# Down projection of a gated feed-forward part: plain blocks and Strassen's seven products, in an encoder trunk of two layers

## The chip, the core and the metric

The kernel runs on one core of one Trainium2 chip. Its time is the device time of one execution in microseconds; the median of three runs before the change is 1561.34 us (1561.25 to 1561.52). The core's engines work side by side and wait for each other by semaphores: TensorE (PE; its weight loads are shown as PEld), VectorE (DVE), ScalarE (ACT), GpSimd (POOL), and SyncE (SP), which here issues nearly all DMAs. Matmuls write their sums into eight PSUM buffers of 128 partitions x 512 float32; the other working memory is SBUF.

## What is computed

The input x has 512 tokens of 1024 channels, and two layers follow each other. Each has three attention or pooling branches, which the change leaves alone, and a feed-forward part:

```python
x = x + merged @ w_out[l]
hf = rms_norm(x, ffn_norm_g[l])
u = depthwise_conv(hf @ ffn_w_up[l], ffn_conv_w[l], ffn_conv_b[l])   # width 3, along the tokens
u_gate, u_val = u[..., :D_FF], u[..., D_FF:]                          # D_FF = 2816
x = x + (jax.nn.silu(u_gate) * u_val) @ ffn_w_down[l]                 # 2816 -> 1024
```

All of it is float32. The kernel keeps that precision by splitting each operand of a matmul into a high part (rounded to TensorE's float32r) and a low part (the remainder), and by adding three matmuls: high x high, high x low, low x high.

## The kernel before

Everything lies transposed: channels on the 128 partitions, the 512 tokens along the row. The residual is the tile `XM` (8 row tiles of 128 channels), its normed and split form `HH` and `HL`.

**Weights.** The host packs all weights into one stream of pieces of up to 512 columns, in the order of use. `w_dma` loads two pieces at a time into one of three buffers `raw` (512 KB, on SP's queue). `w_split` makes of a piece the high part `wh` (a copy on ACT, line 248) and the low part `wl` (a subtraction on POOL, at times on DVE, line 256); `wnext` hands out the next piece and sees to it that three more are prepared.

**Up projection.** 2816 = 22 column tiles of 128 for the gate (part 0) and as many for the value (part 1). Each of the 44 takes 8 x 3 matmuls of 512 columns (`mm3`, line 405) into one PSUM buffer out of six (`acc`, `ST`, `AV`, two each). `up_evac` follows: DVE scales the result by the norm into an SBUF tile `u`; ACT forms the middle tap of the convolution in `a`; DVE adds the two outer taps (two instructions on `a` and `u`, line 260); then comes silu on ACT for the gate, or the product with the gate on DVE for the value, and the split into `ah` (ACT) and `al` (POOL). 22 pairs `ah`, `al` are kept until the down projection.

**Down projection.** For each of 8 row tiles m, 22 x 3 matmuls of 512 columns add up in one buffer; DVE adds the buffer to `XM`, and the result is stored. In layer 0 the next layer's norm is begun on it (`HH` on ACT, `HL` on DVE, squares on ACT, their sum on POOL); in layer 1 it is the output. Only the last row tile of layer 1 is cut into two halves of 256 tokens, in two buffers (`mi`, `S`), so that one half is stored while the other is still computed.

**Order.** Each engine runs its instructions in the order in which the program was written. That order comes from a planner in the program: `chain` lists the steps of one piece of work with what they wait for, and a model of the engines' times (`Clock`, `Engine`) decides how the steps of different chains follow each other.

Of the kernel before, what the change touches and what calls it, by code (L numbers as in the profile page):

```python
# [10 lines left out]
F32 = mybir.dt.float32  # L11
# [30 lines left out]
END = object()  # L42

# [42 lines left out]
def _widths():  # L86
# [10 lines left out]
    return r + [T] * (2 * KC) + [T] * (4 * FC) + [T] * (2 * FC)  # L97

# [191 lines left out]
def trunk(ctx: ExitStack, tc: tile.TileContext, x, w, prm, gb, cst, pad, out):  # L290
# [60 lines left out]
    raws, halves, pool_only = {}, {}, [False]  # L351

# [29 lines left out]

    def pick(bias, t=0.0):
# [9 lines left out]
    def w_ahead(j):  # L393
        while st["split"] <= min(j, len(pieces) - 1):
            w_split()

    def wnext():
        j = st["use"]
        w_ahead(j + LA if j > LA else j)
        st["use"] += 1  # L400
        need(("w", j))
# [28 lines left out]
    MQ, MK = [[cp.tile([P, 4, 4, 96], F32, tag=f"{n}{g}", name=f"{n}{g}") for g in range(2)] for n in ("MQ", "MK")]  # L430
# [144 lines left out]
    def layer(l, sq, xsrc):  # L575
        pr = prms[l]
        G1, G2 = 2 * l, 2 * l + 1

# [1080 lines left out]
        act = {}  # L1659
        gated = {}  # L1660
        fin = {}

        def up_evac(c, part, acc, tag):
            ci = c + part * FC
            u, a = slot("u"), slot("a")

            def scale():
                V.tensor_tensor(u[:, :T], acc, fin["rbc"][:, :T], ALU.mult)
                free(tag)
# [8 lines left out]
                                               ALU.mult, ALU.add)]  # L1678
            if part == 0:
# [4 lines left out]
                steps.append(gate)  # L1684
            else:
                ah, al = slot("ah", F32R), slot("al", F32R)
                act[c] = (ah, al)
# [3 lines left out]
                steps += [([("gate", l, c)], prod), *split(ah[:, :T], al[:, :T], a[:, :T], eng=G),  # L1691
                          lambda: done("act", l, c)]
            chain(*steps)

        n = 0
        norm_begin(G2, sq)
        for c in range(FC):
            for part in range(2):
                tag = tags[n % 3]
                n += 1  # L1700
                acc = ps(tag)
                for i, _ in enumerate(feat_major(acc, G2)):
                    norm_finish(G2, fin, n == 3 and i == 6)
                up_evac(c, part, acc, tag)

        last = l == L - 1
        sq = None if last else slot("sq")
        idx, tail = 0, []
        two = [ps(t) for t in ("mi", "S")] if last else None

        def half(n, kc, wh, wl):
            ts = slice(256 * n, 256 * n + 256)
            mm3(two[n][:, :256], wh, wl, act[kc][0][:, ts], act[kc][1][:, ts], kc == 0, kc == FC - 1)

        def out_half(n):
            ts = slice(256 * n, 256 * n + 256)
# [229 lines left out]
```

## Time and profile before

| | |
|---|---|
| median of three runs | 1561.34 us |
| the profiled execution, and its span | 1560.56 us, 1558.8 us |
| PE busy | 1547.1 us (99%), 7034 matmuls |
| DVE, ACT, POOL busy | 991.3, 790.6, 1038.5 us |
| layer 0: up projection, down projection | 421 to 661.3 us, 661.3 to 781 us |
| layer 1: up projection, down projection | 1195 to 1434.7 us, 1434.7 us to the end |
| granted TensorE clock | 1.0 |

The profile names an instruction by its line in the program, its engine, its output and inputs (buffer numbers left out) and their shapes. Lines of helpers stand for many uses: 405 is every split matmul, 256 every two-operand instruction of DVE or POOL. The rows that matter are shown where they are used.

### The profile page before, as it was taken

How to read it: one execution, taken by the hardware profiler on the slowest of the kernel's cores; microseconds unless marked ns; L12 is line 12 of the kernel's file. 1: busy time of each engine (PE TensorE's matmuls, PEld its weight loads, DVE VectorE, ACT ScalarE, POOL GpSimd, SP SyncE). 2: the span in 40 equal slices, each digit the busy share in tenths (PEclk: the TensorE clock that was granted, in tenths of full speed). 3: DMA queues.
4: the chain of work that ended last, by engine and by line, in shares of the span. 5: the costliest groups of instructions: out<-in, count | busy, mean ns of one | idle time of the engine just before them, and what ended most of it. 6: DMA issues, size and time to landing. Idle time of an engine off the chain costs nothing.

```text
span 1558.8 us, 20414 instructions
## 1 busy us (share of the span) xinstructions
PE 1547.1 (99%) x7034; PEld 1286.1 (83%) x7034; DVE 991.3 (64%) x1470; ACT 790.6 (51%) x1459; POOL 1038.5 (67%) x920
## 2 busy tenths in 40 slices
PE   9999999999999999999999999999999999999999
PEld 8888788888888888888898877888888888888888
DVE  6778889986277777711046788899762877776000
ACT  6557776663444444432244587766533544444221
POOL 4865986854766666664578669878547676666542
PEclk9999999999999999999999999999999999999999
DMA  6432234425323233333335322444243232322331
GB/s 216 122 107 74 75 104 133 130 80 155 101 82 109 95 95 96 94 122 113 110 109 132 109 69 68 128 126 133 79 144 95 95 102 88 108 95 95 108 131 46
DMA packets 82855, 166.46 MB, mean 107 GB/s; under 512 B 20928, under 2 KB 42944, under 8 KB 82752
## 3 DMA queue, kind: packets, MB, share of 16 engines
q1 hardware_dynamic: 82464, 165.03, 34.1%
q8 instruction: 55, 0.90, 0.2%
q14 instruction: 48, 0.39, 0.1%
q10 hardware_dynamic: 288, 0.14, 0.0%
HBM read 151.50 MB, written 13.63 MB: 106 GB/s over the span
## 4 chain that ended last, share of the span: by engine, by line
PE 89%; ACT 3%; DVE 3%; POOL 3%; issue 1%; DMA 0%; SPq 0%; POOLq 0%; ACTq 0%; DVEq 0%
PE ps_acc L405 39%; PE ps_AV L405 22%; PE ps_ST L405 20%; PE ps_S L405 2%; PE ps_mi L405 2%; PE ps_ST L1365 1%; POOL qa L256 1%; DVE XM L256 1%; ACT ps_ST L248 1%; DVE mgl L256 0%; POOL oraw L256 0%; ACT wh L248 0%; PE ps_ST L1323 0%; PE ps_mi L1365 0%; ACT qa L248 0%
## 5 line engine op out<-in xcount | busy, mean ns | idle before, releaser
L256 POOL TENSOR_TENSOR wl<-raw,wh 128x512 fp32r<-128x512 f32 (+3 forms) x501 | 672.3, 1353 | 382.9 <-ACT wh L248 342.0
L248 ACT ACTIVATE wh<-raw 128x512 fp32r<-128x512 f32 (+2 forms) x521 | 309.1, 608 | 128.7 <-PE ps_ST L405 43.5
L260 DVE SCALAR_TENSOR_TENSOR a<-u,prm,a 128x511 f32<-128x511 f32 x176 | 248.5, 1415 | 86.9 <-ACT a L248 80.6
L405 PE MATMUL ps_acc<-HH,wh 128*128 128x512 f32 x592 | 230.9, 390 | 0.0
L405 PE MATMUL ps_acc<-HL,wh 128*128 128x512 f32 x592 | 230.7, 390 | 0.0
L405 PE MATMUL ps_acc<-HH,wl 128*128 128x512 f32 x592 | 230.6, 389 | 0.0
L405 PEld LDWEIGHTS ps_acc<-HH,wl 128*128 128x128 f32 x592 | 111.1, 188 | 23.3
L405 PEld LDWEIGHTS ps_acc<-HH,wh 128*128 128x128 f32 x592 | 111.2, 188 | 23.2 <-DVE gt L256 0.6
L405 PEld LDWEIGHTS ps_acc<-HL,wh 128*128 128x128 f32 x592 | 111.2, 188 | 22.5
L405 PE MATMUL ps_AV<-HH,wh 128*128 128x512 f32 x288 | 112.3, 390 | 0.0
L405 PE MATMUL ps_AV<-HH,wl 128*128 128x512 f32 x288 | 112.1, 389 | 0.0
L405 PE MATMUL ps_AV<-HL,wh 128*128 128x512 f32 x288 | 112.1, 389 | 0.0
L256 POOL TENSOR_TENSOR al<-a,ah 128x512 fp32r<-128x512 f32 x44 | 59.9, 1360 | 76.8 <-ACT ah L248 74.7
L405 PE MATMUL ps_ST<-HH,wh 128*128 128x512 f32 x240 | 93.5, 390 | 0.0
L405 PE MATMUL ps_ST<-HL,wh 128*128 128x512 f32 x240 | 93.4, 389 | 0.0
L405 PE MATMUL ps_ST<-HH,wl 128*128 128x512 f32 x240 | 93.4, 389 | 0.0
L248 ACT ACTIVATE ah<-a 128x512 fp32r<-128x512 f32 x44 | 27.8, 632 | 121.0 <-DVE a L256 121.0
L248 ACT ACTIVATE a<-u,prm 128x512 f32<-128x512 f32 x88 | 71.0, 809 | 26.2 <-DVE u L256 25.5
L248 ACT ACTIVATE a<-a 128x512 f32<-128x512 f32 x44 | 27.6, 632 | 108.8 <-DVE a L260 108.8
L248 ACT ACTIVATE HH<-XM,prm 128x512 fp32r<-128x512 f32 x32 | 23.1, 722 | 102.5 <-DVE XM L256 53.9
L405 PEld LDWEIGHTS ps_AV<-HH,wl 128*128 128x128 f32 x288 | 54.1, 188 | 11.3
L405 PEld LDWEIGHTS ps_AV<-HH,wh 128*128 128x128 f32 x288 | 54.1, 188 | 11.1
(414 smaller groups left out, 3751.0 us busy)
## 6 DMA issues: line engine op xcount, KB each, us to landing
raw<-w SPq DMA_DIRECT2D x228, 512.0 KB, 3.5
raw<-w SPq DMA_DIRECT2D x13, 384.0 KB, 3.0
XM<-x SPq DMA_DIRECT2D x16, 256.0 KB, 3.7
dtq<-tr SPq DMA_DIRECT2D x16, 192.0 KB, 1.9
dtk<-tr SPq DMA_DIRECT2D x16, 192.0 KB, 2.0
tf<-dtq SPq DMA_DIRECT2D x48, 64.0 KB, 2.1
tf<-dtk SPq DMA_DIRECT2D x48, 64.0 KB, 2.3
raw<-w SPq DMA_DIRECT2D x6, 448.0 KB, 3.3
```

Source lines behind the costliest of these rows:

```text
L248: return self.eng.activation(out, in_, func, **k)
L256: return self.eng.tensor_tensor(out, *a)
L260: return self.eng.scalar_tensor_tensor(out, *a)
L405: PE.matmul(o, lhsT=lhsT, rhs=rhs, start=start, stop=stop)
L1365: PE.matmul(sc, lhsT=s[a_][:, kb_], rhs=s[b_][:, :T], start=False, stop=n == len(pairs) - 1, skip_group_check=True)
```

## The change

**Seven products.** Rows and contraction tiles of the down projection are taken in pairs, and the tokens in halves of 256. A piece of weights now holds a 2 x 2 block of 128 x 128 tiles (the host lays it out so). From the four blocks and four blocks of activations (two contraction tiles x two halves of tokens), seven products are formed in place of eight, each as three matmuls of 256 columns (`products`, line 1832 after). They add up over the contraction in four PSUM buffers per row pair; `unite` then forms the sums of the products and adds them to `XM`.

**Sums of weights** (`w_seven`): four of seven left factors are sums of blocks. ACT copies one block into a PSUM buffer (`mi` or `S`, in turn), three DVE instructions (256, 128 and 128 columns) form the sums there, ACT copies the 512 columns to a second `wh`, DVE subtracts for a second `wl`. The first `wh` and `wl` have 384 columns, since the fourth block is used only in sums. Pieces are prepared two ahead (`wnext`).

**Sums of activations** (`up_evac`): for every second column tile, DVE and POOL form the sums of activations, and three tiles of 512 and half of one are split per pair.

**Convolution out of PSUM**: the scaled value stays in the PSUM buffer (`u = acc`) in place of an SBUF tile, and the buffer is freed only behind the outer taps.

**Two halves**: column tiles 0 to 11 go up, and down as a partial sum, then tiles 12 to 21. One up tile of the second half (tile 12, part 0) runs ahead of the first half's products. The tiles `MQ`, `MK` of the attention serve as room for activations. The cut of the last row tile is gone: rows 6 and 7 end together.

```diff
+HALVES = ((0, 12), (12, 22))
+def _ups(c0, c1):
+    r = [(c, part) for c in range(c0, c1) for part in range(2)]
+    return r[c0 > 0:] + ([(c1, 0)] if c1 < FC else [])
...
+    def w_seven():
...
+        s = sums[j % 2]
+        a12, a11, a21 = (r[:, n * P:n * P + P] for n in (0, 2, 3))
+        s1, s2, s4 = (s[:, n * P:n * P + P] for n in (0, 2, 3))
+        def first():
+            A.activation(s2, a21, AF.Copy)
+            done("a21", j)
+            A.activation(his[0][:, :384], r[:, :384], AF.Copy)
+        def rest():
+            e = pick(W_BIAS)
+            e.tensor_tensor(los[0][:, :384], r[:, :384], f(his[0][:, :384]), ALU.subtract)
...
+        def both():
+            V.tensor_tensor(s[:, :256].rearrange("p (a b) -> p a b", a=2), s2[:, None, :].to_broadcast([P, 2, P]),
+                            r[:, P:3 * P].rearrange("p (a b) -> p a b", a=2), ALU.subtract)
+        def third():
+            V.tensor_tensor(s2, a11, s1, ALU.subtract)
+        def fourth():
+            V.tensor_tensor(s4, a12, s2, ALU.subtract)
+        def lo():
+            V.tensor_tensor(los[1], s, f(his[1]), ALU.subtract)
+            done("w", j)
+        chain(([("w", j - 2)] if seven[j - 2] else [], first), rest, after=0.0)
+        chain(([("a21", j)], both), third, fourth, lambda: A.activation(his[1], s, AF.Copy), lo, after=0.01)
...
         def up_evac(c, part, acc, tag):
-            u, a = slot("u"), slot("a")
+            u, a = acc, slot("a")
             def scale():
-                V.tensor_tensor(u[:, :T], acc, fin["rbc"][:, :T], ALU.mult)
-                free(tag)
+                V.tensor_tensor(u, acc, fin["rbc"][:, :T], ALU.mult)
...
+            def turns():
+                eng = V if c + 1 in (HALVES[0][1], HALVES[1][1]) else G
+                w0 = whole.pop(p)
+                chain(diff(t3, b22, w0[:, 256:T], ALU.add), diff(t4, b21, t2), qfree,
+                      *split(new[4][:, :T], new[5][:, :T], t34[:, :T], eng=eng), end(2), after=0.0)
+                chain(*split(new[2][:, :T], new[3][:, :T], t12[:, :T], eng=eng), end(1), after=0.0)
+            w0 = whole[p]
+            chain(([("first", l, p)], lambda: G.tensor_tensor(t1, w0[:, 256:T], w0[:, :256], ALU.subtract)), after=0.5)
+            chain(*steps, ([("gate", l, c)], prod), diff(t2, b22, t1, ALU.add), turns,
+                  *split(new[0][:, :T], new[1][:, :T], q), lambda: (done("act", l, p, 0), qfree()))
+        def products(kp, m, banks_, first):
...
+            bank_ = {2: (0, 0), 3: (0, 1), 1: (1, 0), 6: (1, 1), 4: (2, 0), 5: (2, 1), 7: (3, 0)}
+            left_ = {1: (0, 2), 2: (0, 0), 3: (1, 3), 4: (0, 1), 5: (1, 0), 6: (1, 2), 7: (1, 1)}
...
+            for n in (2, 1, 3, 6, 5, 4, 7):
...
+                for q, (x_, y_) in enumerate(((lh, rh), (lh, rl), (ll, rh))):
+                    PE.matmul(o, lhsT=x_, rhs=y_, start=first and b not in seen and q == 0, stop=False, skip_group_check=True)
...
+        def unite(m, banks_, then):
...
+            rush = then is not None and l == L - 1 and m == KC - 2
+            e = V if rush else G
+            chain(lambda: A.activation(p1, b1[:, :256], AF.Copy), after=0.0)
+            chain(add(x0, x0, b0), lambda: free(t0), add(u2, p1, b1[:, hi_]), lambda: free(t1),
+                  add(x0[:, hi_], x0[:, hi_], b2[:, hi_]), add(x1, x1, b2), lambda: free(t2),
+                  add(u3, u2, b3[:, :256]), lambda: free(t3),
+                  add(x0, x0, u[:, :T], e), lambda: then and then(m),
+                  lambda: e.tensor_tensor(pair(x1), pair(x1), u3[:, None, :].to_broadcast([P, 2, 256]), ALU.add),
+                  lambda: then and then(m + 1), after=0.0)
...
+        for c0, c1 in HALVES:
+            for c, part in _ups(c0, c1):
...
+            for m in range(0, KC, 2):
+                banks_ = {}
+                for k in range(c0, c1, 2):
+                    products(k // 2, m, banks_, k == c0)
+                unite(m, banks_, finish if c1 == FC else None)
```

**How the order moves.** TensorE, the first matmuls of layer 0's down projection, before: each takes the 512 columns of one activation tile, and 66 in a row go into one buffer (`ps_acc_6580`; `ah`, `al` are the parts of a column tile, `wh`, `wl` those of the weights).

```order
L405 MATMUL ps_acc_6580<-ah_4721,wh_6512 128x512
L405 MATMUL ps_acc_6580<-al_4722,wh_6512 128x512
L405 MATMUL ps_acc_6580<-ah_4721,wl_6513 128x512
L405 MATMUL ps_acc_6580<-ah_4813,wh_6512 128x512
L405 MATMUL ps_acc_6580<-al_4814,wh_6512 128x512
L405 MATMUL ps_acc_6580<-ah_4813,wl_6513 128x512
```

The same place in the change, the first four products of the first half (`sMK`, `sMQ` are activations in the attention's old room; `wh_0` and `wl_0` are the blocks as they are, `wh_1` and `wl_1` the sums; x2 stands for two halves of one tile).

```order
L1832 MATMUL ps_ST_5810<-sMK_4635,wh_0_5701 128x256
L1832 MATMUL ps_ST_5810<-sMK_4634,wh_0_5701 128x256
L1832 MATMUL ps_ST_5810<-sMK_4635,wl_0_5703 128x256
L1832 MATMUL ps_AV_5816<-sMK_4635,wh_0_5701 128x256 x2
L1832 MATMUL ps_AV_5816<-sMK_4635,wl_0_5703 128x256
L1832 MATMUL ps_ST_5810<-sMK_4635,wh_1_5702 128x256
L1832 MATMUL ps_ST_5810<-sMK_4634,wh_1_5702 128x256
L1832 MATMUL ps_ST_5810<-sMK_4635,wl_1_5704 128x256
L1832 MATMUL ps_AV_5816<-sMK_4634,wh_1_5702 128x256 x2
L1832 MATMUL ps_AV_5816<-sMK_4634,wl_1_5704 128x256
```

One matmul over 512 columns has become matmuls over 256 that go round four buffers; in all 990 wide and 132 narrow ones give way to 1848 narrow ones. The sums of weights are needed from the third product on.

VectorE behind layer 0's second up stage, in the change: `ps_ST_7538` is the last product of gate and value, `t_910`, `t_911` the sums of activations, `ah` the low parts of their splits, `ps_mi` and `ps_S` the sums of weights; `wl_1_7592` is the low part of the sums of piece 3, counted from 0.

```order
L272 TENSOR_TENSOR ps_ST_7538<-a_7537,a_7494 128x512
L272 TENSOR_TENSOR ps_mi_4767<-raw_7454,ps_mi_4767 128x128
L272 TENSOR_TENSOR t_910_7539<-ps_ST_7538,t_910_7539 128x256
L272 TENSOR_TENSOR ps_mi_4767<-raw_7454,ps_mi_4767 128x128
L272 TENSOR_TENSOR t_911_7540<-ps_ST_7538,a_7439 128x256
L272 TENSOR_TENSOR ps_S_4768<-ps_S_4768,raw_7454 128x256
L272 TENSOR_TENSOR t_911_7540<-ps_ST_7538,t_910_7539 128x256
L272 TENSOR_TENSOR ps_S_4768<-raw_7454,ps_S_4768 128x128
L272 TENSOR_TENSOR ah_7544<-t_910_7539,ah_7543 128x512
L272 TENSOR_TENSOR ps_S_4768<-raw_7454,ps_S_4768 128x128
L272 TENSOR_TENSOR ah_7542<-ps_ST_7538,ah_7541 128x512
L272 TENSOR_TENSOR wl_1_7592<-ps_mi_4767,wh_1_7590 128x512
```

Ahead of these rows stand, counted from the scaling of the last up tile: the sums of piece 2 (256, 128, 128 columns), the two outer taps of the last tile, the `wl` of piece 2, and the first sum of piece 3 (256). Before the change, nothing of the weights stood on VectorE at this place; only the convolution and the last product did.

VectorE at the end of the program, before:

```order
L256 TENSOR_TENSOR XM<-ps_acc_14078,XM 128x512
L256 TENSOR_TENSOR XM<-ps_ST_14173,XM 128x512
L256 TENSOR_TENSOR XM<-ps_AV_14272,XM 128x512
L256 TENSOR_TENSOR XM<-ps_acc_14367,XM 128x512
L256 TENSOR_TENSOR XM<-ps_mi_13780,XM 128x256
L256 TENSOR_TENSOR XM<-ps_S_13781,XM 128x256
```

And in the change, from the last sum of weights on (`ps_AV_16284` holds the seventh product, the last to be computed; `u_1868`, `u_1869` are the sums of products):

```order
L272 TENSOR_TENSOR wl_1_16329<-ps_S_12909,wh_1_16327 128x512
L272 TENSOR_TENSOR XM<-XM,ps_AV_16257 128x512
L272 TENSOR_TENSOR u_1868_16405<-u_1868_16405,ps_acc_16262 128x256
L272 TENSOR_TENSOR XM<-XM,ps_ST_16275 128x256
L272 TENSOR_TENSOR XM<-XM,ps_ST_16275 128x512
L272 TENSOR_TENSOR u_1869_16406<-u_1868_16405,ps_AV_16284 128x256
L272 TENSOR_TENSOR XM<-XM,u_1868_16405 128x512
L272 TENSOR_TENSOR XM<-XM,u_1869_16406 128x512
```

Where one half-width addition stood behind the last matmul, three additions (256, 512 and 512 columns) and the rest of a fourth now do, and the last store is a whole row tile.

More of the change, by code (lines that the diff above doesn't have):

```diff
@@ L351, in trunk @@
     raws, halves, pool_only = {}, {}, [False]
+    seven, sums = _seven(), []
     def w_dma():
@@ new lines, in layer, with finish @@
+        last = l == L - 1
+        ring = ("acc", "ST", "AV")
+        turn_, n = [0], 0
+        norm_begin(G2, sq)
+        sq = None if last else slot("sq")
+        def finish(m):
+            SY.dma_start(out[m] if last else xsp[m], XM[:, m, :])
+            if not last:
+                chain(*norm_steps(G2 + 1, m, prms[l + 1][:, PRM_AG + m:PRM_AG + m + 1], sq), after=0.0)
+        for c0, c1 in HALVES:
+            room[:] = spare
+            for c, part in _ups(c0, c1):
+                tag = ring[turn_[0] % 3]
+                turn_[0] += 1
```

180 lines of the change are left out of this document (111 added, 69 removed).

## Prediction

> **What bounds the kernel now.** I read the page first: shares by engine, then the chain of work that ended last.
>
> ```profile
> span 1558.8 us, 20414 instructions
> PE 1547.1 (99%) x7034; PEld 1286.1 (83%) x7034; DVE 991.3 (64%) x1470; ACT 790.6 (51%) x1459; POOL 1038.5 (67%) x920
> PE 89%; ACT 3%; DVE 3%; POOL 3%; issue 1%; DMA 0%; SPq 0%; POOLq 0%; ACTq 0%; DVEq 0%
> ```
>
> TensorE holds the chain; no wait for data, and no DMA, carries as much as 4%. A busy PE in this profile need not be a PE at its peak, so the next view is the table by stage: layer 0's up projection, its down projection, then layer 1's down projection with the tail.
>
> ```profile
> 421.00:661.30 240.30, 240.30 (x1063) 199.00 (x1062) 170.12 (x157) 107.12 (x175) 163.56 (x112) 1.00 0.31 97
> 661.30:781.00 119.70, 119.70 (x530) 99.12 (x529) 14.50 (x19) 35.30 (x61) 63.75 (x51) 1.00 0.35 112
> 1434.70:1558.80 124.10, 120.78 (x596) 102.53 (x594) 9.78 (x13) 27.25 (x44) 54.04 (x42) 0.99 0.29 95
> ```
>
> The columns are length, then busy time (and count) of PE, PEld, DVE, ACT and POOL, then clock, DMA share, GB/s. In the down stage PE has no gap, its clock is 1.00, and VectorE works 14.5 of 119.7 us. So the stage lasts what its matmuls last, and VectorE, ScalarE and GpSimd have room there. The change trades exactly this: fewer matmul columns against sums on those engines.
>
> The price of a matmul is its spacing, not its duration (0.39 and 0.28 us overlap). The timeline of PE in layer 1's down stage gives both widths, first and last row of each series:
>
> ```profile
> 1499.82 0.39 PE L405 MATMUL ps_ST<-ah,wl 128*128 128x512 f32 x1
> ...
> 1521.58 0.39 PE L405 MATMUL ps_AV<-ah,wl 128*128 128x512 f32 x1
> ```
> ```profile
> 1539.60 0.28 PE L405 MATMUL ps_mi<-al,wh 128*128 128x256 f32 x1
> ...
> 1555.20 0.28 PE L405 MATMUL ps_S<-ah,wl 128*128 128x256 f32 x1
> ```
>
> 96 steps in 21.76 us: **0.2267 us** for 512 columns. 130 steps in 15.60 us (second to last of 132 matmuls): **0.1200 us** for 256. The narrow form thus costs 53% of the wide one, not 50%.
>
> **PE, term by term.** Before, the two layers' down projections are 2 x 8 x 22 x 3 = 1056 products' worth; 66 of them (the last row tile) already run as 132 halves: 990 x 0.2267 + 132 x 0.1200 = 240.3 us. After: per layer 4 row pairs x 11 contraction pairs x 7 products x 3 split terms = 924 matmuls of 256 columns, 1848 in all, as the instruction order confirms: 1848 x 0.1200 = 221.8 us. **Gain 18.6 us**, 7.7% of the stage: of Strassen's 12.5%, about 5 points go to the dearer narrow form. Up projections keep their matmuls, so they give and take nothing.
>
> The Trainium skill ("TensorE: Matmul & The Clock Gate", section Back-to-back issue gap) gives N/2.4 + 2.5 ns, so 109 ns for 256 columns and 216 ns for 512. By it the gain would be 26 us instead of 18.6. The rows above are slower than that at both widths, and the sum stays with the rows.
>
> **Sums of weights.** A piece (2 x 2 blocks of weights) feeds 21 matmuls, 2.52 us. Nearest rows for its instructions:
>
> ```profile
> L256 DVE TENSOR_TENSOR pl<-ps_ST,ph 128x512 fp32r<-128x512 f32 x74 | 49.6, 681 | 5.2 <-ACT ph L248 4.1 <-POOL wl L256 0.3
> L256 DVE TENSOR_TENSOR rp<-ps_AV,tabg 128x256 f32<-128x256 f32 x8 | 3.0, 416 | 1.1 <-ACT gqs L248 1.1
> L282 DVE STREAM_TRANSPOSE tr<-gqr 128x128 f32<-128x128 f32 x24 | 5.2, 273 | 0.0
> L248 ACT ACTIVATE ph<-ps_ST 128x512 fp32r<-128x512 f32 x36 | 21.7, 603 | 0.6
> L248 ACT ACTIVATE wh<-raw 128x384 fp32r<-128x384 f32 x23 | 11.6, 519 | 3.7 <-PE ps_ST L405 2.2 <-issue 0.6 <-POOL wl L256 0.5
> L248 ACT ACTIVATE qb<-nmt 32x128 fp32r<-32x128 f32 x32 | 9.9, 308 | 9.3 <-DVE nmt L282 8.7
> L256 POOL TENSOR_TENSOR wl<-raw,wh 128x384 fp32r<-128x384 f32 x15 | 15.1, 1014 | 10.0 <-ACT wh L248 8.2 <-issue 1.3 <-PE ps_ST L405 0.5
> ```
>
> VectorE: 0.42 + 2 x 0.27 + 0.68 = 1.64 us; ScalarE: 0.31 + 0.52 + 0.60 = 1.43; GpSimd: 1.01. All lie under 2.52, and the pieces are prepared two ahead (5.04 us). In a row the chain takes 0.31 + 0.42 + 0.54 + 0.60 + 0.68 = 2.6 us plus handoffs of some 0.04. So they cost nothing while nothing else stands in VectorE's queue; the cover is the 5.04 us of lead. Where it runs out, PE waits for a piece's second half, which it first needs 0.72 us into the piece.
>
> **Where other work stands in that queue.**
>
> ```profile
> L260 DVE SCALAR_TENSOR_TENSOR a<-u,prm,a 128x511 f32<-128x511 f32 x176 | 248.5, 1415 | 86.9 <-ACT a L248 80.6 <-POOL wl L256 3.2
> L260 DVE SCALAR_TENSOR_TENSOR vt<-ps_ST,vg,vt 128x512 fp32r<-128x512 f32 x32 | 23.4, 732 | 0.0
> L256 DVE TENSOR_TENSOR XM<-ps_acc,XM 128x512 f32<-128x512 f32 x6 | 4.1, 691 | 73.4 <-PE ps_acc L405 73.4
> L260 DVE SCALAR_TENSOR_TENSOR HL<-XM,prm,HH 128x512 fp32r<-128x512 f32 x32 | 24.0, 751 | 20.2 <-ACT HH L248 20.1
> L256 POOL TENSOR_TENSOR XM<-XM,gt 128x512 f32<-128x512 f32 x16 | 20.7, 1295 | 3.4 <-DVE gt L260 3.3 <-PE ps_ST L1365 0.2
> ```
>
> In the up stage the convolution now reads its input from PSUM. The closest row of that form took 0.73 where the one from SBUF took 1.42, so VectorE gets lighter there: 176 x 0.69 = 121 us of its work go (bounds 0 and 121). PE had no gap in that stage, so this buys no time, only room for the new sums of activations (3 x 0.42 + 0.68 = 1.9 us a column pair, which PE takes 21.8 for).
>
> *(a) From up to down, four times.* By the order of the second half, the sum `wl` of piece 3 stands behind the convolution, product, sums and splits of the last column tile. VectorE's first step after the up stage began 0.4 us behind it and took 0.69:
>
> ```profile
> 661.70 0.69 DVE L256 TENSOR_TENSOR u<-ps_ST,rbc 128x512 f32<-128x512 f32 x1 [0.22 <-PE ps_ST L405]
> ```
>
> From there to the end of that `wl` stand two 0.73, five of 512 columns (0.68 or 0.69), six of 256 (0.42) and six of 128 (0.27): 1.1 + 9.0 = 10.1 us. PE wants it at 3 x 2.52 + 0.72 = 8.3. That is 1.8 late. Instructions that don't depend on each other started 0.61 apart instead of 0.69:
>
> ```profile
> 590.40 0.69 DVE L256 TENSOR_TENSOR a<-a,a 128x512 f32<-128x512 f32 x1
> 591.01 0.68 DVE L256 TENSOR_TENSOR u<-ps_acc,rbc 128x512 f32<-128x512 f32 x1
> ```
>
> With up to 1.4 us saved so, 0.4 to 1.8 late; I take 1.0, about the middle. The first halves have a spare up tile (5.44 us) ahead of the products, but its own convolution too; the same value. Four times 1.0: **+4.0** (0 to 7).
>
> *(b) Between row pairs, 12 times.* A pair fills four of six PSUM buffers, so the next pair's third buffer is the last one's first. It is wanted after four products, 1.44 us; the addition that frees it takes 0.69 behind at most one 0.68. The fourth is wanted at 2.16 and freed some 1.1 us behind that. I take 0.15 each: **+1.8** (0 to 5).
>
> *(c) Layer 0's second half.* Per pair VectorE has 5 x 1.64 + 2 x 0.69 + 3 x 0.42 = 10.8 us of 12.6; in layer 0 two `HL` of 0.75 of the next norm come on top: 12.3 of 12.6. A queue that full lets some pieces be late: **+1.5** (0 to 5). GpSimd, with 5 x 1.01 and four full ones at 1.30, has 10.2, ScalarE, with 5 x 1.43 and five more of 0.6, about as much.
>
> *(d) The tail.* Before, the last matmul is followed by one half-width addition (0.42) and a 128 KB store:
>
> ```profile
> 1555.52 0.42 DVE L256 TENSOR_TENSOR XM<-ps_S,XM 128x256 f32<-128x256 f32 x1 [0.65 <-PE ps_S L405]
> 1555.97 0.35 ACTq L1718 DMA_DIRECT2D out<-XM  x1
> ```
> ```profile
> out<-XM SPq DMA_DIRECT2D x7, 256.0 KB, 2.2
> out<-XM ACTq DMA_DIRECT2D x1, 128.0 KB, 1.7
> ```
>
> After, behind the last matmul there are the rest of one full addition (0.3), one of 256 (0.42), two full ones (0.69 each), and a 256 KB store: 2.1 - 0.4 + 0.5 = 2.2, with handoffs **+2.3** (1.8 to 3).
>
> *(e) At nothing:* the weight DMAs are the same bytes in the same queue; a 512 KB tile now lasts 5.04 us instead of 5.44, three are in flight, and one landed in 3.5 us:
>
> ```profile
> raw<-w SPq DMA_DIRECT2D x228, 512.0 KB, 3.5
> ```
>
> Stores of XM wait at the same place in SyncE's queue as before, with a weight load behind them; without that cover a late one would cost a piece's wait of a few us. The next layer wants the last two `HH` tiles only behind six others (8 x 12 narrower matmuls), so the later residual is hidden too.
>
> **Sum.** -18.6 + 4.0 + 1.8 + 1.5 + 2.3 = **-9.0 us**. The profiled execution took 1560.56 (span 1558.8 and 1.8 around it), so 1551.6; the runs' median, 1561.34, lies 0.8 above it. I give 1552.3 for the median.
>
> **Rivals.**
> 1. *The waits hardly show.* VectorE overlaps its instructions everywhere, (a) to (c) stay under 3 us together. For: PE hid everything in the old down stage. Against: 86% to 98% of VectorE's time is planned. 1544.5 to 1547. Chance 0.11.
> 2. *VectorE is the bound in layer 0's second half.* `HL` reads two SBUF tensors while GpSimd works; the convolution with that form took 1.42. Then a pair is 12.3 + 1.3 = 13.6 against 12.6, 4 us in four pairs, 2.5 more than in (c), and with (a) at 1.8 each 3.2 more: 1558 to 1559. Against: `HL`'s own row is 0.75. Chance 0.14. The Trainium skill ("SBUF — State Buffer", section Who interferes with whom) states that a VectorE instruction with two SBUF inputs and a GpSimd one that reads SBUF shut each other out. It would speak for this rival; the 1.42 and 0.73 rows agree, the 0.75 row doesn't show it.
> 3. *Slower: the chain of weight sums sets the pace.* Its intermediate sums sit in two PSUM banks, so a chain may take at most 5.04 us from first copy to last subtraction. It decides against the change from 5.41 us (0.185 more per piece times 88 is the 16.3 left behind the tail). At 6 us it costs 88 x 0.48 = 42: 1587. For: six steps over two engines with foreign work between. Against: alone 2.6 us plus handoffs, and at a row pair at most 2.6 us of other VectorE work. Chance 0.08.
> 4. *Narrow matmuls as cheap as columns alone.* If 0.1200 came from two alternating banks, and the new order over four runs at half of 0.2267 (0.1133), 12.4 us more are gained: 1540. But the two series differ by 0.1067 us for 256 columns, which leaves 13 ns a matmul whatever its width, in wide ones that run on one bank too. Chance 0.03. The Trainium skill's formula, above, would give 7.6 of these 12.4 us.
>
> **How the numbers follow.** The forecast (1547 to 1557) has 0.64. Low end 1545, into rivals 1 and 4; high end 1559, half of rival 2; outside stays some 0.2. A difference of 0.2% (3.1 us) is about what a measurement of this kernel can tell from no change. Faster: 0.64 + 0.11 + 0.03 + a part of rival 2 (0.06) = 0.84; same 0.08; slower 0.08.
>
> **What would show it.** PE's 256-wide spacing in the down stages 0.120; gaps of PE of about 1 us in the third or fourth piece behind each up stage, released by `wl` on DVE; small gaps in front of the third buffer of a row pair; the convolution at 0.73; VectorE near full in layer 0's second half; 3.4 us between the last matmul and the last store. Wrong would be the spacing, or waits for `wl` inside the pairs.

## The result, and the profile after

The change makes the kernel faster by 9.3 us: median 1552.14 us (1551.67 to 1552.46) against 1561.43 us (1561.25 to 1561.99) of the kernel before, measured beside it; ratio 0.994, 95% interval 0.9922 to 0.9957. The profiled execution took 1551.91 us.

The page of the changed kernel, the same lines as of before (span; busy time of each engine; shares of the chain that ended last):

```profile
span 1550.1 us, 22862 instructions
PE 1531.9 (99%) x7760; PEld 1307.6 (84%) x7760; DVE 1090.8 (70%) x1986; ACT 870.7 (56%) x1695; POOL 1031.7 (67%) x983
PE 87%; DVE 5%; ACT 3%; POOL 3%; issue 1%; DVEq 0%; POOLq 0%; ACTq 0%
```

PE is still busy for 99% of the span, with 15 us less of it; VectorE has some 100 us and ScalarE 80 us more work. Little of that shows in the chain: VectorE's share went from 3% to 5%.

The table by stage of the change (length; busy time and count of PE, PEld, DVE, ACT, POOL; clock; DMA share; GB/s): layer 0's first up half, its first down half, second up half, second down half.

```profile
422.60:558.90 136.30, 136.30 (x604) 112.88 (x603) 79.35 (x121) 66.58 (x113) 87.14 (x73) 1.00 0.32 97
558.90:621.20 62.30, 60.93 (x505) 60.52 (x504) 45.59 (x113) 32.85 (x80) 34.43 (x32) 1.00 0.34 102
621.20:724.60 103.40, 103.40 (x458) 85.65 (x457) 57.80 (x90) 49.55 (x86) 66.34 (x58) 1.00 0.32 97
724.60:775.80 51.20, 50.62 (x421) 50.40 (x420) 46.62 (x105) 33.73 (x76) 33.17 (x30) 1.00 0.40 125
```

The up halves have no gap on PE. In the down halves it has small ones (62.30 - 60.93 and 51.20 - 50.62 us; the modelled end of a matmul covers the first few tenths of each gap), and VectorE, almost idle there before, now works 46 of 62 and 47 of 51 us. What PE waits for in its down halves is in the table of waits (us in total, times, longest):

```profile
PE ps_ST L1832 <- ACT wh L264: 2.3, 2, 1.1
PE ps_AV L1832 <- DVE wl L272: 1.2, 2, 0.6
PE ps_acc L470 <- DVE u L272: 0.7, 1, 0.7
...
PE ps_ST L1832 <- DVE wl L272: 0.4, 2, 0.2
```

"2 times" is once in each layer. The first and the last row belong to one piece, the third of the first halves; the second row is the fourth piece of the second halves. The third row is no wait of a down half: it is the start of the next layer. A wait in this table begins at the modelled end of the matmul before it, so it is some 0.2 us shorter than the time that PE loses from start to start.

The start-up of the program, the same instructions in both, took 421.9 and 422.6 us. From the first up matmul on, by the starts of stages on PE's timeline (before the change, the first up matmul starts at 421.9 and the first down matmul at 661.5, a little behind the round figures used so far):

| | before | after | difference |
|---|---|---|---|
| layer 0, up | 239.6 | 136.3 + 103.4 | 0.0 |
| layer 0, down | 119.7 | 62.4 + 51.2 | -6.1 |
| layer 1, to its first down matmul, and its second up half | 653.6 | 551.6 + 103.4 | +1.4 |
| layer 1, down, to the start of the last matmul | 120.4 | 62.4 + 51.1 | -6.9 |
| from there to the end | 3.6 | 5.8 | +2.2 |
| sum | 1136.9 | 1127.5 | -9.4 |

### The profile page after: what moved, and what is told of

It reads as the page before. It is cut to its first block, busy times and chain, and to the rows that moved or that the text cites. A ratio compares the mean times of both kernels' runs of the same rounds, so it can differ in the third digit from the quotient of the medians.

```text
span 1550.1 us, 22862 instructions
## 1 busy us (share of the span) xinstructions
PE 1531.9 (99%) x7760; PEld 1307.6 (84%) x7760; DVE 1090.8 (70%) x1986; ACT 870.7 (56%) x1695; POOL 1031.7 (67%) x983
## 4 chain that ended last, share of the span: by engine, by line
PE 87%; DVE 5%; ACT 3%; POOL 3%; issue 1%; DVEq 0%; POOLq 0%; ACTq 0%
PE ps_acc L470 34%; PE ps_AV L470 19%; PE ps_ST L470 15%; PE ps_AV L1832 5%; PE ps_ST L1832 5%; PE ps_acc L1832 4%; PE ps_S L470 2%; PE ps_mi L470 2%; PE ps_ST L1430 1%; POOL qa L272 1%; DVE XM L272 1%; ACT ps_ST L264 1%; DVE mgl L272 1%; POOL oraw L272 0%; ACT wh L264 0%
## 5 line engine op out<-in xcount | busy, mean ns | idle before, releaser
L272 POOL TENSOR_TENSOR wl<-raw,wh 128x512 fp32r<-128x512 f32 (+3 forms) x498 | 608.6, 1229 | 403.6 <-ACT wh L264 378.2
L264 ACT ACTIVATE wh<-raw 128x512 fp32r<-128x512 f32 (+2 forms) x521 | 300.9, 590 | 31.4 <-DMA raw<-w 12.0
L470 PE MATMUL ps_acc<-HH,wh 128*128 128x512 f32 x608 | 237.2, 390 | 0.2
L470 PE MATMUL ps_ST<-HH,wl 128*128 128x512 f32 x224 | 87.1, 389 | 0.0
L470 PEld LDWEIGHTS ps_AV<-HL,wh 128*128 128x128 f32 x288 | 54.1, 188 | 10.9
L276 DVE SCALAR_TENSOR_TENSOR a<-ps_acc,prm,a 128x511 f32<-128x511 f32 x64 | 47.9, 748 | 21.4 <-ACT a L264 20.5
L1832 PE MATMUL ps_ST<-ah,wh 128*128 128x256 f32 x278 | 55.5, 284 | 2.3 <-ACT wh L264 2.3
L276 DVE SCALAR_TENSOR_TENSOR a<-ps_AV,prm,a 128x511 f32<-128x511 f32 x56 | 42.0, 749 | 21.3 <-ACT a L264 20.3
L276 DVE SCALAR_TENSOR_TENSOR a<-ps_ST,prm,a 128x511 f32<-128x511 f32 x56 | 41.9, 749 | 20.0 <-ACT a L264 19.2
L264 ACT ACTIVATE gt<-gt 128x512 f32<-128x512 f32 x48 | 30.2, 628 | 45.3 <-DVE gt L272 45.1
```

What stands on the lines that cost most here:

```text
L264: return self.eng.activation(out, in_, func, **k)
L272: return self.eng.tensor_tensor(out, *a)
L276: return self.eng.scalar_tensor_tensor(out, *a)
L470: PE.matmul(o, lhsT=lhsT, rhs=rhs, start=start, stop=stop)
L1832: PE.matmul(o, lhsT=x_, rhs=y_, start=first and b not in seen and q == 0, stop=False, skip_group_check=True)
```

## The experiments

The theory: the gain is TensorE's, 18.5 us from columns that are no longer computed, and it is paid down by VectorE's queue only where the down stage begins and at the two ends of the layers, not inside. The rivals: the sums of weights hold up the pieces throughout; or the convolution out of PSUM, which rides along, is part of the gain. The start-up varies by up to 2 us from kernel to kernel (421.1 to 423.3), so small differences are read from the first up matmul to the end of the span, 1127.5 us in the change.

### The price of the narrow form

In the kernel before, each product of 512 columns in the down stage becomes two of 256:

```diff
-                    mm3(acc, wh[:, ws], wl[:, ws], act[kc][0][:, :T], act[kc][1][:, :T], kc == 0, kc == FC - 1)
+                    for ts in (slice(0, 256), slice(256, T)):
+                        for q, (x_, y_) in enumerate(((wh, 0), (wh, 1), (wl, 0))):
+                            PE.matmul(acc[:, ts], lhsT=x_[:, ws], rhs=act[kc][y_][:, ts], ...)
```

> The kernel before, with every matmul of the down projection cut into two of 256 columns and no Strassen (990 wide ones become 1980 narrow ones). My theory: the narrow form costs 0.1200 against 0.2267 whatever the scheme, so 1980 x 0.1200 - 990 x 0.2267 = +13.2 us: about 1574.6, and Strassen's seventh then saves 264 x 0.1200 = 31.7 of it. Rival (narrow matmuls cost only their columns, and the change lost its gain elsewhere): about 1561 to 1564.

Measured: 1574.28 us, ratio 1.0083 (1.0069 to 1.0097), 13.1 us more. Its down stage of layer 0:

```profile
661.80:788.50 126.70, 126.70 (x1058) 126.70 (x1057) 14.32 (x18) 35.30 (x61) 64.18 (x51) 1.00 0.35 107
```

1056 matmuls in 126.7 us are 0.120 each, with 14 us of VectorE work beside them and in one buffer at a time. PEld, the weight loads, fills the stage too: 126.7 of 126.7, where the wide form had 99 of 120. So 0.120 belongs to the narrow matmul with its weight load, not to the order over buffers or to waits for sums. Which of the two sets it, the matmul or its load, these runs don't tell apart. Half of the wide form's price, 0.1133, was reached in neither order.

### The sums of weights left out

ACT copies all 512 columns to PSUM and the three sums on VectorE are left out; the down projection is computed with other weights, all matmuls and transfers remain:

```diff
-            A.activation(s2, a21, AF.Copy)
+            A.activation(s, r, AF.Copy)
...
-        chain(([("a21", j)], both), third, fourth, lambda: A.activation(his[1], s, AF.Copy), lo, after=0.01)
+        chain(([("a21", j)], lambda: A.activation(his[1], s, AF.Copy)), lo, after=0.01)
```

> The change without the three sums of weights per piece: the second high and low parts are made of the blocks themselves, so the down projection's result is another one; ScalarE copies 512 columns instead of 128 for it, VectorE loses 1.0 of 1.7 us per piece. My theory: inside the pieces the sums cost TensorE nothing, and only the four waits behind the up stages (5.4 us) shrink: 1547 to 1549. Rival (the sums hold TensorE back throughout): 10 us or more less than 1552.

Measured: 1545.91 us, ratio 0.9902 (0.9889 to 0.9916), from the first up matmul to the end 5.7 us less than the change. Its down halves of layer 0:

```profile
558.20:618.70 60.50, 60.50 (x506) 60.50 (x505) 27.10 (x47) 38.65 (x79) 34.52 (x32) 1.00 0.35 105
722.00:772.40 50.40, 50.40 (x421) 50.36 (x421) 34.77 (x52) 38.12 (x76) 36.02 (x32) 1.00 0.41 132
```

504 and 420 matmuls at 0.120 are 60.48 and 50.40: PE has nothing to wait for. The sums cost the change 2.7 us a layer in its down halves, and the wait at the layer change is gone with them. This is about what an arrangement of the sums can win back: some 6 us.

### The spare tile's evaluation put off

One up tile runs ahead of the first down half so that PE has work; its scaling and taps on VectorE stand in front of the sums of the third and fourth pieces. Here its chain may be put 9 us later:

```diff
-                chain(*steps, gate)
+                chain(*steps, gate, after=9.0 if c == HALVES[0][1] else 0.2)
```

> The change, with the convolution of the spare up tile (tile 12, part 0) begun 9 us later, so that it no longer stands on VectorE ahead of the sums of piece 2. My theory: the wait of 1.9 us behind each first up stage is VectorE's queue order, and both go: 3.8 us less, about 1548.4. Rival (the chain of the weight sums itself is too long for its lead): the wait stays, 1552.

Measured: 1548.81 us, ratio 0.9921 (0.9907 to 0.9934); first up matmul to end 1124.9, 2.6 less than the change, where 3.8 were expected. Why it helps is seen in the change's timeline of DVE and ACT behind the first up stage (start, length in us), where the spare tile is `ps_acc`:

```profile
560.61 0.69 DVE L272 TENSOR_TENSOR ps_acc<-ps_acc,rbc 128x512 f32<-128x512 f32 x1
...
561.80 0.42 DVE L272 TENSOR_TENSOR ps_S<-ps_S,raw 128x256 f32<-128x256 f32 x1
...
562.73 0.74 DVE L276 SCALAR_TENSOR_TENSOR a<-ps_acc,prm,a 128x511 f32<-128x511 f32 x1
563.39 0.28 DVE L272 TENSOR_TENSOR ps_S<-raw,ps_S 128x128 f32<-128x128 f32 x1
...
564.58 0.28 DVE L272 TENSOR_TENSOR ps_S<-raw,ps_S 128x128 f32<-128x128 f32 x1
564.75 0.63 ACT L264 ACTIVATE a<-a 128x512 f32<-128x512 f32 x1 [2.03 <-DVE a L276]
565.29 0.58 ACT L264 ACTIVATE wh<-ps_S 128x512 fp32r<-128x512 f32 x1
```

The chain of piece 2, counted from 0 (`ps_S`), needs 1.0 us of VectorE and takes from 561.80 to 564.86, because a split, the first sum of piece 3 and the spare tile's taps (the second is among the rows left out) stand between its steps. The ACT copy that PE waits for comes behind, and not at once: the spare tile's silu (`a<-a`) stands in front of it on ScalarE, so the copy starts at 565.29, some 0.4 us behind the last sum. So the spare tile is in the way in two queues, and the edit moves it out of both. With the spare tile later, the first half takes 60.8 us instead of 62.3; the second half, which has no spare tile, is unchanged at 51.2:

```profile
558.70:619.50 60.80, 60.70 (x506) 60.49 (x504) 45.81 (x113) 32.78 (x80) 34.87 (x32) 1.00 0.33 104
```

What is left over the matmuls' 60.5 us is no longer at the entry. In front of the third buffer of the second row pair, PE now loses 0.35 us in layer 0 and 0.65 in layer 1 (its first half takes 61.1), until an addition to `XM` on VectorE frees the buffer. That is the place of the prediction's term (b), which is empty in the change itself.

### And the last splits on GpSimd

In addition, the splits of the last tile of a half go to GpSimd (`G`) like all others:

```diff
-                eng = V if c + 1 in (HALVES[0][1], HALVES[1][1]) else G
+                eng = G
```

> The change with the spare tile's evaluation put off, as before, and the last splits of activations of both halves on GpSimd in place of VectorE (two of 0.68 us in front of the low part of piece 3). Theory (PE waits behind an up stage only because VectorE's queue holds the last tile's work in front of a piece's low part): the 0.82 us wait of layer 0's second half, and its like in layer 1, go; 1.6 us less than with the spare tile put off alone, from the first up matmul to the end 1123.3. Rival (the splits, late on GpSimd at 1.0 us each, hold up the last product of a half, or the low parts of the first 384 columns, which GpSimd also does): PE waits for al or for wl on POOL in place of DVE, and the time stays or grows by 1 to 2 us.

Measured: **1547.59 us**, ratio 0.9911 (0.9898 to 0.9925), the fastest complete version of the study; first up matmul to end 1123.3, the number that the theory gave. Its two down halves of layer 0:

```profile
558.90:619.60 60.70, 60.70 (x506) 60.54 (x505) 44.56 (x112) 32.87 (x80) 36.21 (x34) 1.00 0.34 103
723.00:773.70 50.70, 50.58 (x421) 50.37 (x420) 44.62 (x103) 33.55 (x76) 35.46 (x32) 1.00 0.42 127
```

No row of `wl` or `wh` is left among PE's waits in the down halves, though PE still loses 0.4 us from start to start at the fourth piece of each second half. Two subtractions of 0.68 us were worth 0.5 us of PE in each layer's second half, 0.9 us in all. The theory had put the whole 1.6 us there. The other 0.7 came from the first halves (now 60.65 us in both layers), where the wait at the second row pair went too. So the place is confirmed, and the exact sum is partly luck.

### One piece ahead instead of two

```diff
-        ... held + 1 + seven[n + 1] <= (LA + 3 if any(seven[j:n + 2]) else LA + 1):
+        ... held + 1 + seven[n + 1] <= LA + 1:
```

> The change, with pieces of the down projection prepared one ahead instead of two. A chain of weight sums takes 2.8 us alone, and a piece's second half is wanted 0.72 us into the piece, so the lead falls from 5.76 to 3.24 us. My theory: the two-piece lead is the cover that makes the sums free; without it TensorE waits in most of the 88 pieces, 0.3 to 1.0 us each: 1575 to 1640. Rival (the chain has ample room): 1552 to 1556.

Measured: 1575.25 us, ratio 1.0091 (1.0076 to 1.0106), 23 us above the change, at the lower edge. Its first down half of layer 0 (the second took 61.8 us), and PE's main waits in all four:

```profile
557.90:625.80 67.90, 64.06 (x506) 63.38 (x505) 48.09 (x117) 33.58 (x82) 33.27 (x31) 0.95 0.28 86
```
```profile
PE ps_ST L1832 <- ACT wh L264: 7.9, 3, 3.6
PE ps_AV L1832 <- DVE wl L272: 3.7, 9, 0.8
```

The same instructions, only prepared later: the waits spread over many pieces (the second row's over nine). The expectation had waits in most of the 88 pieces; the table has 27 of them in the down halves. The dearest half is layer 0's second, 10.6 us longer than in the change, where VectorE is fullest. The 5.04 us of lead is what hides the chain, as the prediction assumed; the sum of VectorE's work is not what decides.

### The two ends

Two edits that aim at the layer change and at the tail. The next layer's first four buffers are taken in another order, and row tiles 6 and 7 get a chain of their own; in the last pair, row 6's sum runs on GpSimd and row 7 is added and stored in two halves on two queues:

```diff
-        ltags = ("acc", "acc", "ST", "ST")
+        ltags = ("acc", "ST", "acc", "ST")
...
+                def store(n):
+                    (SY, nc.scalar)[n].dma_start(out[m + 1][:, 256 * n:256 * n + 256], x1[:, 256 * n:256 * n + 256])
+                chain(add(x0, x0, b0), lambda: free(t0), add(u2, p1, b1[:, hi_]), lambda: free(t1),
+                      add(x0[:, hi_], x0[:, hi_], b2[:, hi_]), fork, add(x1, x1, b2), lambda: free(t2),
+                      add(u3, u2, b3[:, :256]), lambda: free(t3),
+                      add(x1[:, :256], x1[:, :256], u3), lambda: store(0),
+                      add(x1[:, hi_], x1[:, hi_], u3), lambda: store(1), after=0.0)
```

> The change, with two ends reordered. At the end of layer 0 the buffers that the next layer takes first are emptied first, and its first products go to acc, ST, acc, ST; at the end of the program the sum for row 6 runs on GpSimd beside VectorE, and row 7 is added and stored in two halves on two queues. My theory: 0.6 to 1.0 us at the layer change (of 1.0 lost there) and 0.5 to 0.9 at the tail (of 2.2): about 1550.6. Rival (GpSimd and VectorE shut each other out at the tail, and the next layer waits for something else): 1552.

Measured: 1550.95 us, ratio 0.9934 (0.9921 to 0.9946). Its start-up happened to take 421.1 us; from the first up matmul to the end it needs 1127.5 us, exactly the change's. In the timeline of its tail the two half additions take 1.06 us; in the change the two full ones together took 1.28 (the rows are shown below):

```profile
1544.21 1.06 DVE L272 TENSOR_TENSOR XM<-XM,u 128x256 f32<-128x256 f32 x2
```

The first half addition takes 0.73 us of the 1.06, the second 0.41: the first starts while GpSimd's sum of row 6 is running, from 1543.39 to 1544.66. So the rival had a part here, that VectorE and GpSimd hold each other up. From the start of the last matmul to the end it takes 5.7 us, against 5.8. At the layer change the gap fell from 0.97 to 0.25 us, yet from the layer's start to its first down matmul it took 551.7 us, against 551.6: the attention that follows took the time back. Where in it was not traced to the end.

With the late spare tile beside it:

> Both edits, the late convolution of the spare tile and the reordered ends. If their places are apart, the gains add: 3.8 + 1.5 = 5.3 us less, about 1546.8; if the waits only move, 1550 to 1552.

Measured: 1548.72 us, ratio 0.9921 (0.9907 to 0.9934): the late spare tile's gain and nothing more (first up matmul to end 1125.3).

### The convolution out of SBUF

In the change, the scaled value goes to an SBUF tile again, as before:

```diff
-            u, a = acc, slot("a")
+            u, a = slot("u"), slot("a")
...
...
-                V.tensor_tensor(u, acc, fin["rbc"][:, :T], ALU.mult)
+                V.tensor_tensor(u[:, :T], acc, fin["rbc"][:, :T], ALU.mult)
+                free(tag)
...
-                lambda: free(tag)]
```

> The change with the convolution's input back in an SBUF tile, as before it. My theory: the convolution out of PSUM buys no time in the up stages, only room on VectorE, so the outer taps go back to about 1.4 us each and the waits behind the up stages grow by what four such taps add ahead of the weight sums, 1 to 3 us each: 1556 to 1563, all of it in the first pieces of the down stages. Rival (it is no part of the effect): 1552.

Measured: 1589.01 us, ratio 1.0177 (1.0163 to 1.0191): 37 us above the change, far from what either theory gave. The tap's group, two of PE's waits, and the first down half of layer 0:

```profile
L276 DVE SCALAR_TENSOR_TENSOR a<-u,prm,a 128x511 f32<-128x511 f32 x176 | 221.6, 1262 | 82.8 <-ACT a L264 79.6
```
```profile
PE ps_ST L1832 <- ACT wh L264: 8.5, 4, 3.8
...
PE ps_acc L470 <- POOL wl L272: 2.5, 6, 0.6
```
```profile
563.20:631.90 68.70, 63.66 (x505) 62.78 (x505) 50.07 (x121) 35.94 (x82) 35.64 (x33) 0.95 0.32 97
```

The up halves became longer (139.9 and 104.7 us, by the waits for `wl` on POOL), but most of it lies in the down halves: 6.3 us in layer 0's first and 7.9 in its second, 6.5 in both of layer 1. My reading was that the last tiles' slow taps stand in front of the first sums. The next but one tests it.

### The convolution out of PSUM alone

The kernel before, with the reverse edit and nothing else of the change:

> The kernel before with the convolution read out of PSUM, and nothing else of the change. The prediction said that this part buys no time in itself, only room on VectorE: taps at 0.73 to 0.75 us in place of 1.42, VectorE 121 us less busy, and the time 1561.3 within 1.5, since PE has no gap in the up stage. Rival (PE's up stage was held by VectorE where the profile's modelled ends hide it, or the buffer that is now kept some 3 us longer is missing): off by more than 3 us, either way.

Measured: 1560.83 us against 1560.82, ratio 0.9999 (0.999 to 1.0008). Busy times from its page:

```profile
PE 1547.8 (99%) x7034; PEld 1287.5 (83%) x7034; DVE 880.7 (57%) x1470; ACT 792.0 (51%) x1459; POOL 1000.0 (64%) x920
```

VectorE lost 110.6 us of work (taps of 0.75 us), and the time stayed. By itself this part gains nothing; with the sums of weights behind it, it is worth 37 us.

### The convolution out of SBUF, but not next to a down half

```diff
+            near = c + 1 in (HALVES[0][1], HALVES[1][1]) or (c, part) == (HALVES[0][1], 0)
-            u, a = acc, slot("a")
+            u, a = acc if near else slot("u"), slot("a")
...
```

> The change with the convolution out of SBUF in all up tiles but those next to a down half (the last two of each half and the spare tile). Theory A (of the 37 us that the convolution out of SBUF costs everywhere, some 28 arise at the four entries into a down half, where taps of 1.3 to 1.4 us stand in front of the first sums of weights and the long waits bring the clock down): the down halves come back to 62.4 and 51.2 us and the time is about 1560; the rest, some 8 us, stays in the up stages, where PE waits for the low part on POOL. Theory B (VectorE is behind over many tiles, and the delay is carried into the down halves however light the last tiles are): the halves stay at 65 us and 56 us or more and the time above 1575.

Measured: 1583.47 us, ratio 1.0143 (1.013 to 1.0157). My theory A fell; B holds. Layer 0's first up half and its two down halves:

```profile
421.90:562.80 140.90, 138.15 (x603) 112.35 (x602) 100.70 (x115) 64.76 (x111) 99.91 (x73) 1.00 0.29 93
562.80:630.00 67.20, 62.73 (x505) 61.89 (x504) 49.53 (x120) 35.54 (x82) 34.97 (x33) 0.97 0.32 96
734.80:790.90 56.10, 52.88 (x421) 52.06 (x420) 49.59 (x112) 37.98 (x84) 36.48 (x33) 0.97 0.37 116
```

VectorE is busy 101 of 141 us in the up half, so it isn't the sum of its work. But each engine's queue is in order, and VectorE now falls behind from tile to tile: at every fourth tile, from the scaling at 468.0 on, it begins 2.3, 3.9, 4.0 and 4.0 us behind PE's end of that tile. In the change it is 0.2 us each time. How late it is when the down stage comes can be read at the scaling of the last up tile (the tile before the spare one). PE ends that tile 5.44 us ahead of the first down matmul: at 553.4 in the change, at 557.4 here. VectorE begins to scale it, in the change and here:

```profile
553.62 0.70 DVE L272 TENSOR_TENSOR ps_ST<-ps_ST,rbc 128x512 f32<-128x512 f32 x1 [1.66 <-PE ps_ST L470]
```
```profile
560.88 0.69 DVE L272 TENSOR_TENSOR ps_ST<-ps_ST,rbc 128x512 f32<-128x512 f32 x1
568.39 0.69 DVE L272 TENSOR_TENSOR ps_acc<-ps_acc,rbc 128x512 f32<-128x512 f32 x1
...
572.37 0.29 DVE L272 TENSOR_TENSOR ps_S<-raw,ps_S 128x128 f32<-128x128 f32 x1
```

In the change it had waited 1.66 us for PE and starts 0.2 behind it. Here it starts 3.5 behind, without having waited; the spare tile's scaling comes at 568.39 (560.61 in the change), and the last sum of piece 2 at 572.37. PE stands still for 3.7 us. What the PSUM source gives is that slack, 1.66 us at this tile, by which VectorE is never behind when the down stage begins. A lighter last tile doesn't make up for it.

## Why the prediction was right, point by point

**Sum and sign.** -9.4 us between the profiled executions' like stretches, -9.0 predicted; 1552.14 against 1552.3 us. Part of that is luck: two terms that were too high, by 3.3 us together, cover two that were too low or missing, by 2.8.

**TensorE: right.** Where no wait disturbs it, as without the sums, a down half lasts 504 and 420 times 0.120 us. The prediction's own terms, 240.3 - 221.8, make 18.5 us and not 18.6. Rival 4 is excluded: this and the narrow form in the old order run at the same 0.120. The gain that the Trainium skill's formula ("TensorE: Matmul & The Clock Gate", Back-to-back issue gap) would have given, 26.3 us and so 7.8 more (the prediction has 7.6), did not come: the runs stay at 120 ns where it has 109.

**Prices of the sums: right.** Groups of VectorE in the change:

```profile
L272 DVE TENSOR_TENSOR wl<-ps_mi,wh 128x512 fp32r<-128x512 f32 x44 | 30.3, 688 | 17.5 <-ACT wh L264 15.3 <-PE ps_ST L1832 1.4 <-ACT HH L264 0.7
L272 DVE TENSOR_TENSOR ps_S<-raw,ps_S 128x128 f32<-128x128 f32 x88 | 25.8, 293 | 2.0
L276 DVE SCALAR_TENSOR_TENSOR a<-ps_acc,prm,a 128x511 f32<-128x511 f32 x64 | 47.9, 748 | 21.4 <-ACT a L264 20.5
```

0.69, 0.29 and, for the tap, 0.75 against 0.68, 0.27 and 0.73. That they hide inside the pieces was right; rival 3 is excluded, since without the sums only the waits at the entries go.

**(a) Right stage, a little low.** 1.89 us in the first halves (62.37 - 60.48) and 0.82 in the second (51.22 - 50.40), 5.4 us in four against 4.0. In the second halves the place is the one that was worked out, the `wl` of piece 3. The prediction took the same value for the first halves, and there the place was another: the spare tile's evaluation, named as its "own convolution", stands in the chain of piece 2, and PE waits for that piece's `wh` already, over twice as long. The late spare tile and the splits on GpSimd take away 1.5 and 0.5 us of them and so show which work it was. Two readings behind the 1.8 us were off, too. PE wants `wl` with the third matmul of a product, at 8.5 us and not 8.3. And VectorE began 0.2 us behind the up stage, not 0.4: on PE's timeline the up stage of before ends at 661.5, and the scaling begins at 661.70. With both, the working gives 0 to 1.4 us in place of 0.4 to 1.8, and the 0.82 measured lies in the middle of it.

**(b) Too high.** No gap at a row-pair boundary: 0 against 1.8. The range had 0 as its end; the middle was taken without a row for it. The place is real, though: once the spare tile is put off, 0.35 and 0.65 us of wait turn up there.

**(c) Too high.** In layer 0's second half VectorE is busy 46.62 of 51.2 us, 91%, nearly the 98% reckoned with. And `HL` did stretch where rival 2 had it: of the eight for this half's rows, four took 1.00 to 1.79 us in place of 0.75, two of them behind its end (the mean over all 32 in the program, 859 ns, hides that). Still PE misses nothing behind the entry wait: 0 against 1.5. Two pieces of lead level out a queue that is full only on average; with one, this half was the dearest of the four. So rival 2 is out by its price, with its mechanism seen. Rival 1 is out as well: the waits of (a) alone, 5.4 us, are more than its 3.

**(d) Right.** 2.2 us against 2.3. The sign that was to show it, 3.4 us between the last matmul and the last store, doesn't follow from the prediction's own terms (0.8 before and 1.7 more) and wasn't met: it is 2.6 us, from 1544.32 to 1546.88. The tail of the change:

```profile
1544.32 0.28 PE L1832 MATMUL ps_AV<-ah,wl 128*128 128x256 f32 x1
1545.24 0.41 DVE L272 TENSOR_TENSOR u<-u,ps_AV 128x256 f32<-128x256 f32 x1
1545.57 1.28 DVE L272 TENSOR_TENSOR XM<-XM,u 128x512 f32<-128x512 f32 x2
```

**(e) Wrong by 1.0 us.** "The later residual is hidden too" held for `HH`, but the next layer's second group of matmuls also needs a PSUM buffer, which the last sum of products on VectorE frees. That sum stands behind two subtractions of the next layer's own weights, of 1.09 and 1.64 us, and behind an addition:

```profile
773.59 2.65 DVE L272 TENSOR_TENSOR wl<-raw,wh 128x384 fp32r<-128x384 f32 x2 [1.18 <-ACT wh L264]
775.83 0.34 PE L470 MATMUL ps_acc<-wh,HH 128*128 128x384 f32 x1
776.16 0.67 DVE L272 TENSOR_TENSOR XM<-XM,ps_AV 128x512 f32<-128x512 f32 x1
776.76 0.41 DVE L272 TENSOR_TENSOR u<-u,ps_acc 128x256 f32<-128x256 f32 x1
777.22 0.44 PE L470 MATMUL ps_acc<-wh,HH 128*128 128x384 f32 x1 [0.71 <-DVE u L272]
```

PE stood 0.97 us there. A further 0.4 us of the next layer's attention (the rest of the table's +1.4) wasn't traced, and the edits of the two ends show that a gain at this place need not reach the end.

**The convolution: right in the word, wrong in the weight.** "Buys no time, only room" is exact for the kernel before (0.9999). But the prediction put room down at nothing, and never asked what the change would be without it. Without it, the change would be slower than before: 1589. What the cut into two halves and the spare tile are worth by themselves wasn't run.

## What to carry to other kernels

A sum over busy times says whether work fits; whether it is late is decided by the queue's order at the points where a stage begins, so list what stands in front of the first items that the next stage wants, step by step and on every engine of their chain, and expect the wait there. Work that one can put off or move to another engine at that point is worth more than its own time suggests: here two one-line edits took back 4.2 of the 9.1 us by which the change fell short of TensorE's gain. A mean over the whole program hides what happens at such a point, as that of `HL` did; read the instructions of the stage. And a part that gains nothing by itself may be what the other parts stand on: test it inside the change, not only alone.

## What the runs showed of the hardware

**Waits of PE of some 2 to 4 us cost the clock.** In the kernel with the convolution out of SBUF, windows of the wait for `wh` and of what follows:

```profile
570.60:574.60 4.00, 0.32 (x3) 0.12 (x1) 3.56 (x9) 1.79 (x6) 1.44 (x1) 0.80 0.00 0
574.60:580.00 5.40, 5.28 (x24) 5.06 (x25) 3.84 (x9) 3.03 (x8) 2.00 (x2) 0.52 0.64 187
580.00:586.00 6.00, 6.00 (x53) 6.00 (x52) 3.91 (x10) 3.02 (x9) 2.04 (x2) 1.00 0.33 98
```

The granted clock is 0.52 for the 5.4 us behind it: 24 matmuls recorded, where the next 6.0 us have 53. The wait of 3.56 us with pieces one ahead did the same, but a wait need not be that long: 2.5 us did it in this kernel's second half, and in the kernel with the convolution out of SBUF but not next to a down half it was 1.66 us, half a microsecond behind a wait of 0.58. The waits inside the change's down halves, up to 1.1 us, leave its clock at 1.00. In these cases the half clock lasted 3.4 or 6.8 us. The Trainium skill ("TensorE: Matmul & The Clock Gate", Part 1: The HAM clock gate) states that an idle window of some 3.4 us halves the clock until one busy window has passed; the halving and its length agree with the runs, but the idle time that brought it on was less than 3.4 us in some of them. So the price of a late piece isn't linear: of the 8.2 us that this down half takes beyond its matmuls' 60.5, 5.0 are waits, and the clock accounts for most of the rest.

**VectorE and GpSimd stretch each other.** The same instruction twice, in the change's second down half of layer 0, beside a GpSimd addition and mostly without one:

```profile
742.81 1.29 POOL L272 TENSOR_TENSOR XM<-XM,u 128x512 f32<-128x512 f32 x1
742.87 1.79 DVE L276 SCALAR_TENSOR_TENSOR HL<-XM,prm,HH 128x512 fp32r<-128x512 f32 x1
...
745.51 0.73 DVE L276 SCALAR_TENSOR_TENSOR HL<-XM,prm,HH 128x512 fp32r<-128x512 f32 x1
```

Groups of the stretch from 470 to 560 us, in the change and in the kernel with the convolution out of SBUF but not next to a down half:

```profile
L272 POOL TENSOR_TENSOR wl<-raw,wh 128x512 fp32r<-128x512 f32 x29 | 37.3, 1292 | 15.4 <-ACT wh L264 15.4
```
```profile
L272 POOL TENSOR_TENSOR wl<-raw,wh 128x512 fp32r<-128x512 f32 x31 | 46.5, 1510 | 11.5 <-ACT wh L264 11.5
L276 DVE SCALAR_TENSOR_TENSOR a<-u,prm,a 128x511 f32<-128x511 f32 x30 | 40.3, 1344 | 18.5 <-ACT a L264 18.0
```

GpSimd's `wl` took 1510 ns in place of 1292 beside taps of 1344. In the kernel before, where the source of the convolution is the only difference, it is 1521 and 1294 ns in the same stretch. That agrees with the Trainium skill ("SBUF — State Buffer", Who interferes with whom), which lets a VectorE instruction with two SBUF inputs contend with a GpSimd one that reads SBUF. It is the likely reason why PE there waits for `wl` on POOL in the up stage.
